# A planner's estimate of TensorE time: a larger charge for each streamed product and each transpose

## The chip, the cores and the metric

The kernel runs on one core of a Trainium2 chip. The core has the engines TensorE (PE, the matrix engine; its loads of stationary operands are shown as PEld), VectorE (DVE), ScalarE (ACT), GpSimd (POOL) and SyncE (SP), and 16 DMA engines. The metric is the device time of one execution in microseconds; less is better.

## What is computed

The reference is a network of two blocks for one sequence of 256 tokens and a width of 2048, in fp32. Cut to its core:

```python
def first_block(x, mem, ...):                      # one layer
    h = rmsnorm(x, g[0])
    y = hybrid_mixer(h, ...)       # h @ w_in; dilated attention, spatial gating, rwkv7 scan; @ w_out
    x = x + rmsnorm(y, g[1])
    h = rmsnorm(x, g[2])
    y = memory_cross_attention(h, rmsnorm(mem, ...), wq, wkv, wo)
    x = x + rmsnorm(y, g[3])
    h = rmsnorm(x, g[4])
    y = conv_ffn(h, ...)           # h @ w_up (11264 columns), conv of width 3, gelu(gate) * val, @ w_down
    return x + rmsnorm(y, g[5])

def second_block(x, c, ctx, c_ctx, ...):           # two layers, tokens x and 256 tokens ctx
    for l in range(2):
        sh_l, sc_l, g_l = split(silu(c) @ w_mod[l] + b_mod[l], 3)       # the modulation; the same for ctx
        hl = xl * (1 + sc_l) + sh_l;  hc = xc * (1 + sc_c) + sh_c
        # hl @ w_in[l], hc @ w_in[l]: short conv, differential attention (softmax - lam * softmax), pool
        out_l = concatenate([y_conv, y_attn, y_pool]) @ w_out[l]
        xl_new = layernorm(ALPHA * xl + g_l * out_l, ...)               # the same for ctx in layer 0
    return xl
```

## The kernel before

**The stream.** All large weights pass once through PE, in the order of the program. They come as pieces of 512 KB (`load_next`, lines 455 to 462, a DMA on SP into a tile `raw`). Each piece is split into two parts: ACT casts it to `whi` (`split_hi`, line 464), DVE subtracts that from the piece and gives `wlo` (`split_lo`, line 472). The activations (`xT`, `yh`/`yl`, `hh`/`hl`, `oT`) are split in the same way. A product of the reference is then three products on PE: whi by both parts of the activation and wlo by the first (`products`, line 535). A moving operand has 256 or 512 columns. A piece is as a rule 24 products. `split_ahead` (line 480) keeps the splits up to three pieces ahead of the products (LK = 3), and the loads up to four pieces ahead of the splits (EK = 4). In a trace all of this stands at line 342, since the class `Engine` passes every instruction through that line; operations are told apart by the names of their tiles.

**The background.** All other work (norms, transposes, attention, rwkv scan, gates, conv, the modulation) is written as Python generators, one queue of them for each lane: a0 to a2 the rwkv chunks, b and c the attention, d the spatial gating, B and C the differential attention, r, t, u and n norms and residuals, w the modulation, and so on. `products` calls `tick` (line 417) after each quarter of a piece, that is after six products. For each lane `tick` emits the next step if the lane's step before has ended by the planner's estimate: `ready[lane] <= clk["P"]`, where `ready` is the estimated end of the last step plus LAG, 0.1 us. The lane w emits a modulation step (on DVE a product and sum `junk` of 1024 columns, and a DMA of `wm`) if DVE's estimated clock is not ahead of PE's by more than WLAG, 0.3 us. `there` (line 426) holds back a step, and a `split_hi`, whose input has not come by the estimate. `until` emits steps without waiting, where the stream itself needs what they make.

**The estimate.** `Meter.note` (line 302) is called for each instruction as it is written. It holds a clock for each engine: an instruction starts at its engine's clock or when its inputs are written and its output is free, if that is later, and ends after `cost` (line 286). The same clocks decide nothing on the chip: they set only the order in which instructions are written into each engine's queue, and the engines execute these queues in order, with semaphores between them.

**Places that are spoken of below.** In the mixer the chunk chain of rwkv: `kn`, `t`, `zrk`, `rl`, `bk`, `ab` are tiles of a chunk on DVE, and `bk<-cons,t` and `bk<-rl,bk` are its small matrix products on PE (a name `bk` also stands for a bank of PSUM). In the second block, `normal0` (line 1981) normalises the rows r of ctx and then of x at the end of layer 0: lane r scales r on ACT (columns 0 to 255) and DVE (the rest); lanes t and n transpose each r on PE (four transposes, `bk<-cons,r`), and ACT then applies scale and shift (`aff<-bk,gb`, two) and casts the two `xT`. The softmax steps of the differential attention (`softmax2`, line 1792) run on ACT (exp into `p`) and DVE (`s`, `p<-p,s,p`), then four transposes `bk<-cons,p` on PE.

Of the kernel before, what the change touches and what calls it, by code (L numbers as in the profile page):

```python
# [10 lines left out]
F32R = mybir.dt.float32r  # L11
# [6 lines left out]
T = 256  # L18
# [250 lines left out]
class Meter:  # L269
# [16 lines left out]
    def cost(s, e, name, aps):  # L286
        n = max(a.free_size() if callable(a.free_size) else a.free_size for a in aps)
        if e == "P":
            if name == "transpose":
                return 0.06  # L290
            o, l, r = aps[:3]
            m, n = l.shape[-1], r.shape[-1]
            return n / 2400 if r.dtype == F32R and n >= T else 4 * max(m, n) / 2400
        return {"V": 0.07 + n / 960, "A": 0.09 + n / 1190, "G": 0.6 + n / 480}[e]

    def table(s, args):
# [1796 lines left out]
```

## Time and profile before

| | us |
|---|---|
| time, median of three runs | 2880.27 (2879.71 to 2881.02) |
| the profiled execution's own time | 2881.7 |
| its span | 2880.0 |
| PE busy | 2831.7 (98%) |
| DVE busy | 2072.1 (72%) |
| ACT busy | 1275.8 (44%) |
| POOL busy | 173.8 (6%) |

The busy time of PE is that of pipelined products whose ends are modelled, so in a stream one reads the distance of their starts. The mean granted clock of PE is 0.993 of full speed over the span; below 1.0 are a few stretches only, near 80 us, near 667 us and at the very end. The order in which the views are read: the page's first part and its chain, the waits of PE, the starts of products in the timeline, and then single stretches.

### The profile page before, as it was taken

To read this page: it belongs to the slowest core of one execution; us is meant where nothing else is said; L and a number is where in the kernel's file an instruction comes from. 1 tells how busy PE (TensorE), PEld (TensorE's weight loads), DVE (VectorE), ACT (ScalarE), POOL (GpSimd) and SP (SyncE) were. 2 spreads that over 40 slices of the span, in tenths; PEclk is the share of its full clock that TensorE was granted. 3 is DMA by queue.
4 is the path that set the end of the run, shared out by engine and by line. 5 is a ranking of instruction groups with operands and counts; after the bars stand their busy time and mean duration, and the time that the engine had idled before them with its cause. 6 is when DMAs were issued, how large, how long until landed. Compare 5 with 4: busy or idle time off the path is not lost.

```text
span 2880.0 us, 53963 instructions
## 1 busy us (share of the span) xinstructions
PE 2831.7 (98%) x22059; PEld 2673.7 (93%) x22059; DVE 2072.1 (72%) x3377; ACT 1275.8 (44%) x2110; POOL 173.8 (6%) x345
## 2 busy tenths in 40 slices
PE   8899999999999999999999999999999999999997
PEld 8789887898999899998899999999999989999996
DVE  6766766787898997888868887885343563776576
ACT  5333335655544445545443554222231463655443
POOL 1001112000000000000100000000010000001001
PEclk9899999999999999999999999999999999999998
DMA  8433337765667886777775334665343453325663
GB/s 268 134 104 105 126 99 251 241 234 187 237 236 242 307 293 223 235 245 271 244 250 179 124 119 169 213 229 182 98 137 117 155 186 107 103 95 182 199 227 132
DMA packets 150857, 538.78 MB, mean 187 GB/s; under 512 B 18240, under 2 KB 18460, under 8 KB 150608
## 3 DMA queue, kind: packets, MB, share of 16 engines
q1 hardware_dynamic: 137808, 494.92, 50.2%
q0 software_dynamic: 12656, 40.37, 5.0%
q8 instruction: 173, 2.83, 0.4%
q14 instruction: 76, 0.62, 0.1%
q10 hardware_dynamic: 144, 0.03, 0.0%
HBM read 528.66 MB, written 6.59 MB: 186 GB/s over the span
## 4 chain that ended last, share of the span: by engine, by line
PE 95%; DVE 2%; DMA 1%; ACT 1%; issue 1%; POOL 0%; SPq 0%; DVEq 0%; ACTq 0%; POOLq 0%
PE acc L342 86%; PE bk L342 10%; DMA raw<-in_w_w_in 1%; DVE wlo L342 1%; ACT whi L342 0%; DVE y L342 0%; DVE res L342 0%; DVE junk L342 0%; DVE zrk L342 0%; ACT junk L342 0%; DVE yg L342 0%; POOL pw L342 0%; POOL R L342 0%; DVE ug L342 0%; DVE zr L342 0%
## 5 line engine op out<-in xcount | busy, mean ns | idle before, releaser
L342 PE MATMUL acc<-xT,whi 128*128 128x256 f32 x8992 | 1581.0, 286 | 13.5 <-ACT whi L342 12.6
L342 PEld LDWEIGHTS acc<-xT,whi 128*128 128x128 f32 x8992 | 1342.1, 192 | 26.6 <-ACT whi L342 13.5
L342 ACT CAST whi<-raw 128x1024 fp32r<-128x1024 f32 x738 | 771.5, 1050 | 906.5 <-PE acc L342 673.0
L342 PE MATMUL acc<-xT,wlo 128*128 128x256 f32 x4496 | 1128.8, 284 | 1.5 <-DVE wlo L342 1.5
L342 DVE TENSOR_TENSOR wlo<-raw,whi 128x1024 fp32r<-128x1024 f32 x738 | 896.8, 1221 | 273.7 <-ACT whi L342 271.2
L342 PEld LDWEIGHTS acc<-xT,wlo 128*128 128x128 f32 x4496 | 800.0, 192 | 2.3 <-DVE wlo L342 2.3
L342 DVE SCALAR_TENSOR_TENSOR junk<-wm,silu 128x1024 bf16<-128x1024 f32 x352 | 421.9, 1220 | 6.3 <-DMA wm<-in_w_mod 5.8
L342 PE MATMUL acc<-whi,xT 128*128 128x256 f32 (+1 forms) x1152 | 284.8, 331 | 0.4 <-ACT xT L342 0.4
L342 PE MATMUL acc<-whi,yh 128*128 128x256 f32 (+1 forms) x768 | 224.5, 319 | 0.0
L342 PEld LDWEIGHTS acc<-whi,xT 128*128 128x128 f32 x1152 | 195.1, 190 | 20.8 <-issue 2.0
L342 PE MATMUL acc<-wlo,yh 128*128 128x256 f32 (+1 forms) x640 | 194.7, 304 | 0.0
L342 PE MATMUL acc<-wlo,xT 128*128 128x256 f32 (+1 forms) x576 | 187.0, 325 | 0.0
L342 PEld LDWEIGHTS acc<-whi,yh 128*128 128x128 f32 x768 | 146.3, 191 | 9.9
L342 PE MATMUL acc<-whi,yl 128*128 128x256 f32 x512 | 144.9, 283 | 0.0
L342 PE MATMUL acc<-wlo,hh 128*128 128x512 f32 x352 | 137.2, 390 | 0.8 <-DVE wlo L342 0.8
L342 PE MATMUL acc<-whi,hh 128*128 128x512 f32 x352 | 137.2, 390 | 0.0
L342 PE MATMUL acc<-whi,hl 128*128 128x512 f32 x352 | 137.0, 389 | 0.0
L342 PEld LDWEIGHTS acc<-wlo,yh 128*128 128x128 f32 x640 | 122.3, 191 | 5.0
L342 PEld LDWEIGHTS acc<-wlo,xT 128*128 128x128 f32 x576 | 109.7, 190 | 7.1
L342 PEld LDWEIGHTS acc<-whi,yl 128*128 128x128 f32 x512 | 98.2, 192 | 0.0
L342 PE MATMUL acc<-whi,oT 128*128 128x512 f32 x256 | 80.6, 392 | 0.6 <-DVE oT L342 0.6
L342 PEld LDWEIGHTS acc<-wlo,hh 128*128 128x128 f32 x352 | 66.1, 188 | 15.0 <-DVE wlo L342 1.5
(347 smaller groups left out, 2612.8 us busy)
## 6 DMA issues: line engine op xcount, KB each, us to landing
raw<-in_w_w_in SPq DMA_DIRECT2D x334, 512.0 KB, 3.6
wm<-in_w_mod SPq DMA_DIRECT2D x192, 512.0 KB, 4.9
raw<-in_w_up SPq DMA_DIRECT2D x176, 512.0 KB, 4.0
raw<-in_w_w_out SPq DMA_DIRECT2D x108, 512.0 KB, 4.4
raw<-in_w_down SPq DMA_DIRECT2D x88, 512.0 KB, 4.7
raw<-in_w_wkv SPq DMA_DIRECT2D x16, 512.0 KB, 5.2
silu<-cond POOLq DMA_DIRECT2D x12, 512.0 KB, 7.7
raw<-in_w_wq SPq DMA_DIRECT2D x8, 512.0 KB, 3.6
```

Source lines behind the costliest of these rows:

```text
L342: return f(*a, **k)
```

## The change

In `cost`, a transpose is charged 0.11 us instead of 0.06, and a product of the stream (fp32r, 256 columns or more) n/2400 + 0.0133 instead of n/2400, so 0.1200 instead of 0.1067 for 256 columns and 0.2266 instead of 0.2133 for 512. The charge of other products (4 x max(m, n)/2400) stays.

```diff
--- before.py
+++ after.py
@@ -287,10 +287,10 @@
         n = max(a.free_size() if callable(a.free_size) else a.free_size for a in aps)
         if e == "P":
             if name == "transpose":
-                return 0.06
+                return 0.11
             o, l, r = aps[:3]
             m, n = l.shape[-1], r.shape[-1]
-            return n / 2400 if r.dtype == F32R and n >= T else 4 * max(m, n) / 2400
+            return n / 2400 + 0.0133 if r.dtype == F32R and n >= T else 4 * max(m, n) / 2400
         return {"V": 0.07 + n / 960, "A": 0.09 + n / 1190, "G": 0.6 + n / 480}[e]
 
     def table(s, args):
```

No instruction of PE, DVE or DMA is added or removed; the order changes. (ACT's queue has two loads of its function tables fewer, 16 where there were 18.) The small products of rwkv, on DVE and PE, in the mixer near 75 to 90 us: `wlo_916`/`wlo_922` belong to `raw_756`, `wlo_946`/`wlo_948` to `raw_825`. DVE before:

```order
L342 TENSOR_TENSOR wlo_904<-raw_726,whi_886 128x1024
L342 TENSOR_TENSOR wlo_916<-raw_756,whi_896 128x1024
L342 TENSOR_SCALAR kn_918<-bk_906 128x4
L342 TENSOR_TENSOR wlo_946<-raw_825,whi_932 128x1024
L342 COPY t_137_806<-kn_918 128x256
L342 TENSOR_SCALAR t_135_804<-t_135_804 128x256
L342 TENSOR_TENSOR wlo_978<-raw_855,whi_964 128x1024
L342 TENSOR_SCALAR t_137_806<-t_135_804,cols,hcol 128x256
L342 TENSOR_TENSOR t_137_806<-zrk_769,t_137_806 128x256
```

DVE now:

```order
L342 TENSOR_TENSOR wlo_908<-raw_726,whi_886 128x1024
L342 TENSOR_SCALAR kn_910<-bk_898 128x4
L342 TENSOR_TENSOR wlo_922<-raw_756,whi_896 128x1024
L342 COPY t_137_806<-kn_910 128x256
L342 TENSOR_SCALAR t_135_804<-t_135_804 128x256
L342 TENSOR_TENSOR wlo_948<-raw_825,whi_932 128x1024
L342 TENSOR_SCALAR t_137_806<-t_135_804,cols,hcol 128x256
L342 TENSOR_TENSOR t_137_806<-zrk_763,t_137_806 128x256
```

COPY t and the t after it moved ahead of the wlo of `raw_825`; they still stand behind that of `raw_756`. PE at the same place, before:

```order
L342 MATMUL acc_794<-xT_322,whi_896 128x256 x2
L342 MATMUL acc_794<-xT_322,wlo_916 128x256
L342 MATMUL acc_794<-xT_322,whi_896 128x256 x2
L342 MATMUL acc_794<-xT_322,wlo_916 128x256
L342 MATMUL bk_980<-cons,t_137_806 128x128 x2
L342 MATMUL acc_795<-xT_322,whi_896 128x256 x2
L342 MATMUL acc_795<-xT_322,wlo_916 128x256
```

PE now:

```order
L342 MATMUL acc_794<-xT_280,whi_886 128x256 x2
L342 MATMUL acc_794<-xT_280,wlo_908 128x256
L342 MATMUL acc_794<-xT_280,whi_886 128x256 x2
L342 MATMUL acc_794<-xT_280,wlo_908 128x256
L342 MATMUL bk_950<-cons,t_137_806 128x128 x2
L342 MATMUL acc_795<-xT_280,whi_886 128x256 x2
L342 MATMUL acc_795<-xT_280,wlo_908 128x256
```

The product `bk<-cons,t` stood six products into the piece of `raw_756` (`whi_896`) and stands now six products into the piece before it (`whi_886`). The next place is ACT in `normal0` for x, at the end of layer 0. Before:

```order
L342 ACTIVATE r_3676_23979<-r_3676_23979,ab_25851 128x256
L342 ACTIVATE aff_25927<-bk_25919,gb_22179 128x256 x2
L342 CAST xT_25928<-aff_25927 128x256
L342 CAST xT_25929<-aff_25927 128x256
L342 CAST whi_25941<-raw_25867 128x1024
L342 ACTIVATE r_3696_24215<-r_3696_24215,ab_25851 128x256
L342 ACTIVATE aff_25953<-bk_25943,gb_22179 128x256 x2
L342 CAST xT_25954<-aff_25953 128x256
L342 CAST xT_25955<-aff_25953 128x256
L342 ACTIVATE r_3714_24447<-r_3714_24447,ab_25851 128x256
L342 CAST whi_25982<-raw_25885 128x1024
```

Now:

```order
L342 ACTIVATE r_3676_23979<-r_3676_23979,ab_25851 128x256
L342 ACTIVATE r_3696_24215<-r_3696_24215,ab_25851 128x256
L342 ACTIVATE aff_25934<-bk_25919,gb_21459 128x256 x2
L342 CAST xT_25935<-aff_25934 128x256
L342 CAST xT_25936<-aff_25934 128x256
L342 CAST whi_25948<-raw_25867 128x1024
L342 ACTIVATE aff_25950<-bk_25927,gb_21459 128x256 x2
L342 CAST xT_25951<-aff_25950 128x256
L342 CAST xT_25952<-aff_25950 128x256
L342 ACTIVATE r_3714_24447<-r_3714_24447,ab_25851 128x256
L342 ACTIVATE aff_25974<-bk_25964,gb_21459 128x256 x2
L342 CAST xT_25975<-aff_25974 128x256
```

Each r came alone between two sets of aff and xT, with a whi beside nearly each of them; now a second r and a second set come before and closer. The last place is DVE in the FFN's up projection, with `U`, `cg`, `cv` the conv's tiles. Before:

```order
L342 TENSOR_TENSOR wlo_8791<-raw_8670,whi_8777 128x1024
L342 SCALAR_TENSOR_TENSOR junk_8815,mpart_5557<-wm_8533,silu_5558 128x1024
L342 TENSOR_TENSOR wlo_8823<-raw_8703,whi_8807 128x1024
L342 SCALAR_TENSOR_TENSOR junk_8849,mpart_5557<-wm_8643,silu_5558 128x1024
L342 TENSOR_TENSOR U_8851<-acc_8575,Rb_7727 128x512
L342 TENSOR_TENSOR U_8852<-acc_8576,Rb_7727 128x512
L342 TENSOR_TENSOR wlo_8865<-raw_8740,whi_8839 128x1024
L342 SCALAR_TENSOR_TENSOR cg_8853<-U_8851,cols,cg_8853 128x255
```

Now:

```order
L342 TENSOR_TENSOR wlo_8847<-raw_8724,whi_8833 128x1024
L342 SCALAR_TENSOR_TENSOR junk_8865,mpart_5557<-wm_8697,silu_5558 128x1024
L342 SCALAR_TENSOR_TENSOR junk_8873,mpart_5557<-wm_8697,silu_5558 128x1024
L342 TENSOR_TENSOR wlo_8881<-raw_8759,whi_8863 128x1024
L342 SCALAR_TENSOR_TENSOR junk_8905,mpart_5557<-wm_8769,silu_5558 128x1024
L342 TENSOR_TENSOR U_8907<-acc_8629,Rb_7761 128x512
L342 TENSOR_TENSOR U_8908<-acc_8630,Rb_7761 128x512
L342 TENSOR_TENSOR wlo_8921<-raw_8798,whi_8897 128x1024
L342 SCALAR_TENSOR_TENSOR cg_8909<-U_8907,cols,cg_8909 128x255
```

Between the same two pieces there stood one `junk` of the modulation; now there are two.

## Rows read from the trace of the kernel before

**Rows 1.** The page: busy time by engine, and the chain that ended last.

```profile
PE 2831.7 (98%) x22059; PEld 2673.7 (93%) x22059; DVE 2072.1 (72%) x3377; ACT 1275.8 (44%) x2110; POOL 173.8 (6%) x345
...
PE 95%; DVE 2%; DMA 1%; ACT 1%; issue 1%; POOL 0%; SPq 0%; DVEq 0%; ACTq 0%; POOLq 0%
```

**Rows 2.** Waits of PE, whole run: waiting engine, releaser, total us, times, longest.

```profile
PE acc L342 <- ACT whi L342: 12.6, 2, 7.0
PE bk L342 <- DVE t L342: 6.2, 1, 6.2
PE bk L342 <- DVE yg L342: 4.6, 4, 3.4
...
PE bk L342 <- DVE y L342: 0.2, 1, 0.2
```

**Rows 3.** Timeline of PE: start, us, engine, operation, count, and idle before it.

```profile
715.99 0.40 PE L342 MATMUL acc<-xT,whi 128*128 128x256 f32 x2
...
716.35 0.40 PE L342 MATMUL acc<-xT,whi 128*128 128x256 f32 x2
...
999.64 0.39 PE L342 MATMUL acc<-wlo,hh 128*128 128x512 f32 x1
999.87 0.39 PE L342 MATMUL acc<-whi,hl 128*128 128x512 f32 x1
```

**Rows 4.** One window: PE, PEld, DVE, ACT, POOL busy, PE's clock, DMA share, GB/s.

```profile
90.00:95.00 5.00, 5.00 (x31) 5.00 (x31) 4.81 (x11) 2.55 (x4) 0.00 (x0) 0.66 0.59 226
```

**Rows 5.** Timeline of PE and then of DVE, 78 to 96 us.

```profile
79.88 0.79 PE L342 MATMUL acc<-xT,whi 128*128 128x256 f32 x2 [5.62 <-ACT whi L342]
...
88.51 1.20 PE L342 MATMUL bk<-cons,t 128*128 128x128 f32 x4 [6.15 <-DVE t L342]
...
90.14 0.63 PE L342 MATMUL acc<-xT,whi 128*128 128x256 f32 x2
...
90.78 0.63 PE L342 MATMUL acc<-xT,whi 128*128 128x256 f32 x2
...
79.86 1.23 DVE L342 TENSOR_TENSOR wlo<-raw,whi 128x1024 fp32r<-128x1024 f32 x1 [10.50 <-ACT whi L342]
81.00 0.15 DVE L342 TENSOR_SCALAR kn<-bk 128x4 f32<-128x4 f32 x1
86.93 1.23 DVE L342 TENSOR_TENSOR wlo<-raw,whi 128x1024 fp32r<-128x1024 f32 x1 [5.78 <-ACT whi L342]
...
91.19 0.41 DVE L342 TENSOR_SCALAR t<-t,cols,hcol 128x256 f32<-128x256 f32 x1
...
95.08 0.42 DVE L342 TENSOR_TENSOR bk<-t,t 64x256 f32<-64x256 f32 x1
```

**Rows 6.** A window in the FFN, with the columns of rows 4.

```profile
720.00:960.00 240.00, 240.00 (x1874) 234.36 (x1874) 215.69 (x305) 119.33 (x146) 1.15 (x2) 1.00 0.71 243
```

**Rows 7.** Timeline of DVE in a softmax step.

```profile
1691.94 1.22 DVE L342 SCALAR_TENSOR_TENSOR junk<-wm,silu 128x1024 bf16<-128x1024 f32 x1
...
1693.08 1.29 DVE L342 TENSOR_REDUCE s<-bk 128x1 f32<-128x512 f32 x2
...
1697.13 0.75 DVE L342 SCALAR_TENSOR_TENSOR p<-p,s,p 128x512 f32<-128x512 f32 x1
```

**Rows 8.** Timeline of PE and then of ACT in normal0 for x.

```profile
2327.05 0.60 PE L342 MATMUL bk<-cons,r 128*128 128x128 f32 x4
2328.89 0.60 PE L342 MATMUL bk<-cons,r 128*128 128x128 f32 x4
...
2327.69 1.02 ACT L342 ACTIVATE aff<-bk,gb 128x256 f32<-128x256 f32 x2 [1.84 <-PE bk L342]
...
2329.21 1.05 ACT L342 CAST whi<-raw 128x1024 fp32r<-128x1024 f32 x1
2330.15 0.60 ACT L342 ACTIVATE r<-r,ab 128x256 f32<-128x256 f32 x1
2330.66 1.01 ACT L342 ACTIVATE aff<-bk,gb 128x256 f32<-128x256 f32 x2
```

## The prediction

> **What bounds the kernel now.** I read the page first: TensorE (PE) is busy 98% of the span and the chain that ended last lies on it for 95% [rows 1]. So only three things can move the time: a wait of PE, a stretch in which PE runs at its lower clock, and work added to PE. The change adds no work to it: the same products and transposes are issued. Then I read the waits of PE [rows 2]: the long ones are 12.6 us on ACT whi (two), 6.2 on DVE t (one) and 4.6 on DVE yg (four), 23.4 together; the ten rows of that view, of which the last has 0.2, sum to 29.1, which is all that a better order could take from waits. Next, whether the new charges are true. In the stream three products of 256 columns start every 0.36 us, 0.12 each, and a product of 512 starts 0.23 after the one before [rows 3]. The old charges were 0.107 and 0.213, the new are 0.120 and 0.227. Four transposes and six products of 512 columns stand between the starts 2327.05 and 2328.89 [rows 8], so the four take 1.84 - 6 x 0.227 = 0.48, which is 0.12 each; charged 0.06 before, 0.11 now. So the planner's PE clock ran some 11% behind PE before and is right now. What hangs on it: a background step is emitted once the estimated end of the step before it (plus LAG) is passed by the PE clock. With a clock that runs faster in estimate, fewer products stand between two steps of a chain on ACT or DVE. The order shows this: between the transposes of two softmax steps stand 48 products where the median was 60, and the separate runs of background work on PE number 309 where they were 293.
>
> **The sum, against the profiled execution (2881.7 us; its span 2880.0; the median of the runs shown is 2880.3, 1.4 below it).** Five terms.
>
> (a) *The starved stretch, 64 to 95 us.* Here PE stands 5.62 us for a whi whose raw piece came late (it starts again at 79.88), and after six products 6.15 us for DVE t [rows 5]. The second wait is a matter of order: on DVE, COPY t stands behind the wlo of the next late piece (86.93), while 18 ready products of the 24 of the piece before stand behind bk<-cons,t on PE. Now COPY t stands one wlo earlier, behind that of 79.86 (after which the next operation begins 1.14 later), and bk<-cons,t is issued 24 products earlier. So PE stops 18 products sooner, 18 x 0.12 = 2.2 us before the old stop at 74.3 (79.88 less 5.62), at 72.1; COPY t comes at 81.0 and PE goes on at 81.3. It then has 42 products. At the low clock three take 90.78 - 90.14 = 0.64; before, work began again at 88.5 and the mean clock of 0.66 in 90 to 95 [rows 4] means half clock up to 93.4, 5 us. So bk<-cons,t and about 21 products go at it, 5 us, and 21 at 0.12, 2.5: PE is at the next piece at about 89. Next late there is bk<-rl,bk, now issued in front of that piece: its inputs are eleven operations of DVE behind the wlo of 86.93, which in the old run take from 91.19 to 95.08 + 0.42, 4.3 us. From 88.07 (the wlo's end) that is 92.4. So PE waits some 3 us and starts the piece at 92.4 and bk<-rl,bk; before, it started it 18 products after the 0.85 of bk<-cons,t from 88.51, at 93.2, and had bk<-rl,bk still to do. **Term: -1** (0.8, and 0.2 of low clock). Bounds -3 (eleven operations at the spacing without that queue) and +5 (PE's clock falls a second time in the new wait: 5 us of half clock, 2.5, and another such wait behind the next late piece).
>
> (b) *The steps of normal0 at the end of layer 0.* ACT works there without a pause: from one aff pair to what follows its two xT 1.52 us, a whi 0.94, an r 0.51 [rows 8], while the planner charges 0.09 + 256/1190 = 0.305 for each operation of 256 columns, so 1.5 for the five of a step that take 2.03. In the old order 6, 9, 12, 12, 12, 9, 12 products of 512 columns stand between the eight groups of transposes of x, 72; now 3, 6, 9, 9, 12, 9, 9, 57. PE goes from the first group to the eighth in 57 x 0.227 + 7 x 0.48 = 16.3 us, before in 19.7. ACT, by its order and from the first group on: 0.64 to the first aff, six aff-and-xT sets 9.1, five r 2.6 (two are done earlier) and four whi 3.8, which is 16.1; at the fifth group it ends at 8.2 where PE comes at 8.05. The eight groups of ctx have 108 products of 256 columns between them where 174 stood: 13.0 + 3.4 = 16.4, and ACT comes out within 0.2 of PE in the same way. **Term: +0.5**, bounds 0 and +4 (each series late by one whi and one set more, 2 us).
>
> (c) *Softmax steps.* The chain from the first s to the end of the last p takes 1697.13 + 0.75 - 1693.08 = 4.8 us [rows 7], and 48 products cover 5.76; 60 covered 7.2. One junk or wlo ahead in DVE's queue costs 1.14 (junk to s, [rows 7]), which makes 5.9, 0.2 too long; two make 7.1, 1.3 too long. There are 40 such steps; I take one in ten with two ahead and let half of these be hidden by other steps: 2 x 1.3 = 2.6 as the upper half, 0 as the lower. **Term: +1**, bounds 0 and +4.
>
> (d) *Short steps of the mixer.* Rwkv and attention steps are placed in quanta of six products, 0.72 us; most stay at 12 products, some fall to 6. No row of before shows such a wait in the steady stream. **Term: +1.5**, two steps late by one quantum, bounds 0 and +4 (six).
>
> (e) *Transitions* between stages (all waits but those on whi and t, 29.1 - 12.6 - 6.2 = 10.3, yg's 4.6 among them [rows 2]). Work that is emitted a little earlier against PE should save part of it; the steps in between are not shorter. **Term: -1.5**, bounds -4 and 0.
>
> Costed at nothing: *the modulation in the FFN.* DVE is busy 215.69 of 240 us [rows 6], 90%. That is the planner's rule seen in the trace: it gives DVE a junk of 1024 columns, charged 1.137 and taking 1.14, whenever DVE's estimated clock is not ahead of PE's, and PE's clock was 11% slow. Now DVE will be filled to nearly 100% until the modulation is done, which comes sooner. What hides it is that a wlo is issued some three pieces (8.6 us) ahead of its products. By the rows' durations DVE falls at most 5 us behind. If that cover goes, the rival below. ACT loads its tables two times fewer; ACT is not on the chain.
>
> Sum: -1 + 0.5 + 1 + 1.5 - 1.5 = +0.5, on the median of 2880.3: **2881 us**.
>
> One rule speaks against the new charge. The rows show 0.120 and 0.227. The Trainium skill, "TensorE: Matmul & The Clock Gate", section "Back-to-back issue gap", gives N/2.4 + 2.5 ns for an isolated product at full clock, an estimate of 0.109 and 0.216, and calls even that too long for a stream of 512 columns (131 ns). By it the new charge would be 10% too long, 48 products would cover 5.2 us instead of 5.76, and term (c) would grow to some +10. The trace does not agree with it here, and the rows decide. For ACT the rows show 0.51 between starts for an r of 256 columns with two column operands. "ScalarE: Activation LUTs", section "What ACT_TABLE_LOAD costs", gives 186 ns + 0.833 N and 93 for each such operand, less an overlap of 93: an estimate of 0.49, which agrees; the planner's 0.305 is what is off, and this rests unchanged.
>
> **Rivals.**
> (1) *Covers too short: slower.* With PE's charge exact and ACT's and DVE's still short (0.305 charged, 0.51 taken), the steps lose the 11% of cover that hid this. For it: ACT without a pause in normal0, the long queue on DVE. Against: the median step of before had over 2 us in hand. Price: normal0 +4, softmax 10 steps x 0.8 = 8, mixer +4, less 1.5 and 1 for (e) and (a): +13.5, 2894. It decides the sign from the point at which the late steps sum to more than the 2.5 us that (a) and (e) give back, and passes the bound of 0.2% at some 8.
> (2) *The starved stretch opens: faster.* If the raw pieces or DVE's inputs come some 3 us sooner with the new order, the new wait stays away and with it the one of 6.15: 6.15 and 1 for the low clock, and 2 more from the transitions: -9, or 2871. For it: the second wait was one of order alone. Against: bk<-rl,bk stands behind a wlo that only a late transfer releases. It decides from the point at which bk<-rl,bk is ready by 89.
> (3) *DVE becomes the bound in the FFN.* If DVE's operations take 3% more than charged, over 480 us that is 14 us, less the 8.6 us of lead: +5.8, 2887. Against: junk charged 1.137 takes 1.14.
> (4) *Nothing to see:* order moves, every wait is replaced by one of its size: 2880 within 3.
>
> **How the numbers follow.** 0.2% is 5.8 us, about what a measurement of this kernel can tell from no change. The forecast, with (4), holds 2875 to 2886 and has a chance of 0.55; rival (1) 0.21, rival (3) 0.06, rival (2) 0.18. So faster by over 0.2% 0.18, within 0.55, slower 0.27. The range runs from 2871.5, the price of (2), to 2893, just short of that of (1), and leaves about 1 in 10 out on each side. The likeliest case's own range is 2875 to 2886.
>
> **What would show it.** In the profile after: one wait of some 9 us on DVE t up to 81 us in place of the waits on whi and t, and one of some 3 on DVE bk up to 92 (a); waits on ACT r or aff below 0.5 us each near the end of layer 0 (b); few waits of a bk on p, in sum under 3 us (c); DVE at 97% or more of the windows 480 to 1000 us and at 60% or less behind, with PE's waits on wlo still in sum under 4 us. The prediction is wrong if PE waits appear in the softmax steps by the dozen, if wlo waits come up in the FFN, or if the low clock spreads to a stretch that ran at 1.00 before.

## The result, and the profile after

The changed kernel takes 2895.68 us (median of five runs, 2893.14 to 2898.49), the kernel before 2880.27 (2879.71 to 2881.02): a ratio of 1.0051, interval 1.004 to 1.0063. It is 15 us slower, and its executions differ by 5 us where those of before differ by 1. The profiled execution (2893.1 us, span 2891.4) is the fastest of the five.

The waits of PE over the whole run, to be set against [rows 2]:

```profile
PE bk L342 <- DVE t L342: 8.7, 1, 8.7
PE acc L342 <- ACT whi L342: 6.7, 1, 6.7
PE bk L342 <- DVE yg L342: 4.5, 4, 3.4
PE bk L342 <- DVE mod L342: 2.7, 1, 2.7
PE acc L342 <- DVE wlo L342: 2.3, 4, 0.8
PE bk L342 <- DVE bk L342: 1.5, 1, 1.5
PE bk L342 <- DVE mq L342: 1.4, 1, 1.4
PE bk L342 <- DVE r L342: 1.0, 3, 0.6
PE bk L342 <- DVE p L342: 1.0, 4, 0.3
```

(Eight smaller rows, 2.8 us together, are left out.) New are mod, bk, r and p; the waits on t and mq grew and one of the two on whi went. All waits together are 33 us, only 4 more than before. So the view of the waits alone does not explain 11 us between the two profiled executions. What does is the start of the same product of the stream in both traces: the 18,672 products stand in the same order in every version, so the difference of two starts, each counted from the beginning of its span, is what was lost up to there. (The last column is the last product; a change within 1 us at a column can be background work that stands on the other side of it.)

| starts, us later | 640th (113 us) | 3000th (656) | 5100th (923) | 6900th (1195) | 7100th (1219) | 8500th (1471) | 11000th (1828) | 15300th (2376) | last |
|---|---|---|---|---|---|---|---|---|---|
| changed - before | 1.2 | 2.3 | 1.6 | 2.9 | 7.3 | 5.3 | 8.3 | 10.7 | 11.2 |
| e1 - before | 5.4 | 7.3 | 7.0 | 8.2 | 10.6 | 8.4 | 9.5 | 9.9 | 10.1 |
| e2 - before | 0.2 | 5.4 | 4.2 | 4.2 | 4.2 | 7.7 | 7.7 | 8.4 | 8.3 |
| e4 - before | 7.7 | 11.1 | 10.5 | 11.6 | 11.8 | 10.0 | 13.1 | 15.5 | 16.0 |
| e7 - before | 6.0 | 13.5 | 13.0 | 13.0 | 13.0 | 10.9 | 11.0 | 11.1 | 11.3 |
| e12 - e11 | 4.7 | 11.7 | 11.2 | 11.2 | 11.2 | 9.3 | 9.3 | 9.4 | 9.6 |
| e13 - e11 | 4.0 | 5.4 | 4.9 | 6.0 | 8.7 | 6.8 | 9.8 | 12.2 | 12.7 |
| e15 - e11 | 4.1 | 3.7 | 3.8 | 3.8 | 3.8 | 3.2 | 3.2 | 3.2 | 3.2 |
| e16 - e11 | 0.6 | 0.6 | 2.0 | 3.8 | 3.8 | 6.1 | 9.1 | 11.5 | 12.0 |
| e14 - e11 | 0.1 | 0.1 | 0.2 | 0.2 | 0.2 | -1.6 | -1.6 | -1.5 | -1.3 |

(The lines of e1 to e16 belong to the experiments below.) In the first line the loss comes in steps: 1.3 in the FFN, 4.3 at one place near 1212 us, 3.0 in the softmax of layer 0, 2.4 in normal0, and 2.0 gained from the FFN's end to the start of the second block. Each step has its place in the trace.

**The modulation's end, 1212 us.** The last steps of the modulation are transposes of `mod` on PE. Timeline of PE, then of DVE (start, us, operation, count, idle before it):

```profile
1211.09 0.28 PE L342 MATMUL acc<-xT,wlo 128*128 128x256 f32 x1
1214.06 0.38 PE L342 MATMUL bk<-cons,mod 128*16 128x128 f32 x1 [2.69 <-DVE mod L342]
...
1211.34 1.22 DVE L342 SCALAR_TENSOR_TENSOR junk<-wm,silu 128x1024 bf16<-128x1024 f32 x1
...
1212.49 1.22 DVE L342 TENSOR_TENSOR wlo<-raw,whi 128x1024 fp32r<-128x1024 f32 x1
1213.63 0.16 DVE L342 TENSOR_TENSOR mod<-mpart 128x16 f32<-128x16 f32 x1
...
1216.54 0.99 DVE L342 SCALAR_TENSOR_TENSOR cg<-U,cols,cg 128x255 f32<-128x255 f32 x2
1217.45 1.00 DVE L342 SCALAR_TENSOR_TENSOR cv<-U,cols,cv 128x255 f32<-128x255 f32 x2
```

DVE has a full queue here and reaches mod some 2.7 us after PE has come to the transpose that needs it. The windows of the FFN say how full that queue is (columns as in [rows 4]; DVE is the third pair, PE's clock the number before the last two):

```profile
720.00:960.00 240.00, 239.19 (x1875) 233.66 (x1874) 231.68 (x338) 116.39 (x144) 1.15 (x2) 1.00 0.77 260
960.00:1210.00 250.00, 250.00 (x1731) 234.43 (x1730) 234.03 (x340) 116.55 (x135) 2.63 (x5) 1.00 0.81 281
1230.00:1330.00 100.00, 100.00 (x748) 96.16 (x748) 68.11 (x89) 54.52 (x72) 3.77 (x7) 1.00 0.62 204
1210.00:1215.00 5.00, 2.31 (x17) 2.11 (x16) 4.93 (x12) 1.12 (x2) 0.00 (x0) 0.86 0.50 176
1215.00:1220.00 5.00, 5.00 (x36) 5.00 (x35) 4.91 (x8) 3.72 (x7) 0.00 (x0) 0.80 0.65 206
```

DVE is busy 231.68 us of 240 where it was 215.69 [rows 6], 97 against 90%, and 68.11 of 100 once the modulation is done. After the wait PE's clock stands below 1.00 in two windows, which makes 4.3 us of a wait of 2.7. DVE is behind its estimate because not every charge of DVE is true. A junk is (1.144 us to the next operation, charged 1.137), but the two operations of cg take 0.91 (1216.54 to 1217.45) where the planner counts 0.73, and 40 such pairs stand between 720 and 960 us: 7 us in 240, or 3%.

**normal0.** PE comes to the transposes of r, and r is not finished (timeline of PE, ACT and DVE, layer 0's end; before, [rows 8]):

```profile
2312.01 0.27 PE L342 MATMUL bk<-cons,r 128*128 128x128 f32 x1
2312.83 0.55 PE L342 MATMUL bk<-cons,r 128*128 128x128 f32 x3 [0.55 <-DVE r L342]
...
2344.74 0.66 PE L342 MATMUL bk<-cons,r 128*128 128x128 f32 x4
...
2344.07 0.61 ACT L342 ACTIVATE r<-r,ab 128x256 f32<-128x256 f32 x1
...
2310.56 0.76 DVE L342 TENSOR_TENSOR xT<-aff,xT 128x256 fp32r<-128x256 f32 x2 [0.74 <-ACT xT L342]
...
2311.24 1.22 DVE L342 TENSOR_TENSOR wlo<-raw,whi 128x1024 fp32r<-128x1024 f32 x1
2312.37 0.41 DVE L342 TENSOR_SCALAR r<-r,ab 128x256 f32<-128x256 f32 x1
```

The r that the group of 2344.74 needs begins on ACT at 2344.07 and takes 0.61: it ends 0.06 before. That group loses 0.25 us. The three groups that lose most (those of 2312.01, 2350.65 and 2353.62, 1.7 together) wait for DVE's part of r instead: DVE stands 0.74 us for an xT of ACT, takes a wlo, and comes to r at 2312.37 only. **Softmax.** The same on DVE, where a junk stands before the first reduction; the transposes of p break in two (timeline of DVE, then PE). Before, a junk stood there too [rows 7]; what is new is that fewer products follow.

```profile
1675.46 1.22 DVE L342 SCALAR_TENSOR_TENSOR junk<-wm,silu 128x1024 bf16<-128x1024 f32 x1
...
1676.61 1.28 DVE L342 TENSOR_REDUCE s<-bk 128x2 f32<-128x512 f32 x2
...
1681.59 0.41 PE L342 MATMUL bk<-cons,p 128*128 128x128 f32 x2
...
1682.28 0.44 PE L342 MATMUL bk<-cons,p 128*128 128x128 f32 x2 [0.28 <-DVE p L342]
```

Four transposes that took 0.48 with the way in and out take 1.24, and the view of the waits counts only 0.28 of it. Of the 24 steps of layer 0 seven are late, by 0.07 to 0.91 us, which makes the 3.0.

**The starved stretch.** PE stands once, on t, until 81.03, and then 1.5 us on bk (PE, then DVE; before, [rows 5]):

```profile
81.03 1.19 PE L342 MATMUL bk<-cons,t 128*128 128x128 f32 x4 [8.70 <-DVE t L342]
90.97 1.16 PE L342 MATMUL bk<-rl,bk 64*128 64x128 f32 x8 [1.48 <-DVE bk L342]
...
91.29 0.42 DVE L342 TENSOR_TENSOR bk<-t,t 64x256 f32<-64x256 f32 x1
```

### The profile page after: what moved, and what is told of

Same layout as the page of the kernel before. It is cut to its first block, busy times and chain, and to the rows that moved or that the text cites. A ratio compares the mean times of both kernels' runs of the same rounds, so it can differ in the third digit from the quotient of the medians.

```text
span 2891.4 us, 53960 instructions
## 1 busy us (share of the span) xinstructions
PE 2838.8 (98%) x22059; PEld 2674.1 (92%) x22059; DVE 2067.6 (72%) x3377; ACT 1273.2 (44%) x2108; POOL 181.7 (6%) x345
## 5 line engine op out<-in xcount | busy, mean ns | idle before, releaser
L342 DVE SCALAR_TENSOR_TENSOR junk<-wm,silu 128x1024 bf16<-128x1024 f32 x352 | 420.7, 1218 | 11.5 <-DMA wm<-in_w_mod 10.6
L342 PEld LDWEIGHTS acc<-whi,xT 128*128 128x128 f32 x1152 | 195.1, 190 | 21.4 <-issue 2.7
```

Source lines behind the costliest of these rows:

```text
L342: return f(*a, **k)
```

## The experiments

Theory A: each step of a chain had more products in front of it than its chain took, only because PE was charged too little; with PE right and ACT and DVE still charged too little, the steps come late. Theory B: it is the modulation alone, which now fills DVE. Theory C: any other order costs so much. Theory D: the loss is in the starved stretch. Times are medians with the lowest and highest; ratios are against the kernel before on the same chip.

**The two halves, e1 and e2.**

```diff
-                return 0.11        # e1: transposes back
+                return 0.06
-            return n / 2400 + 0.0133 if ...        # e2: products back
+            return n / 2400 if ...
```

> Only the product's charge (n/2400 + 0.0133); a transpose is charged 0.06 as before. Theory A (each place loses cover, because products that stood between two steps of a chain are gone): nearly the whole loss, since all covers are counted in products: 2892 to 2896, with the waits on mod near 1214 us, on p in the softmax steps and on r in normal0. Theory B (DVE filled up by the modulation): the same, since the products are what moves PE's clock in the FFN. Theory C (chance of the order: any other order moves the time by so much, either way): anything between 2875 and 2895, with waits at other places.

> Only the transpose's charge (0.11); a product is charged n/2400 as before. Theory A: a step with four transposes loses 0.2 us of cover, a tenth of what the products take: 2880 to 2883. Theory B: no transposes stand in the FFN, so nothing: 2880. Theory C: anything between 2875 and 2895.

e1: 2892.31 (2890.55 to 2895.22), ratio 1.0041, with 2.1 us on mod. e2: 2890.03 (2887.65 to 2894.66), ratio 1.0035, without a wait on mod or p, and 0.2 us on r. By theory A the transposes should have cost 1 us and cost 9: in e2's trace 4.2 before the FFN, 2.7 of them at a wait of 2.0 on ACT oT, and 3.5 at the start of the second block (a wait of 2.3 us on ACT xT). The halves sum to 20 where both together cost 15. e1 has the time that A gave, but not the places: 7.0 of its 10.1 us are lost before the FFN, 1.1 in the softmax and 0.4 in normal0, with no wait on r. So cover counted in products explains mod in e1, and it explains neither e2 nor the mixer; this miss is only partly cleared up below.

**The modulation, e3 and e4.** e3 lets the modulation fill DVE to 90% only, by a second clock; e4 puts the transposes of mod off.

```diff
+                s.v2 = max(s.v2, t) + 1.11 * c                      # e3, for each DVE operation
-        if ... not s.quiet and m["V"] <= m["P"] + WLAG:
+        if ... not s.quiet and s.meter.v2 <= m["P"] + WLAG:
+        t1 = s.meter.last + 4.0                                     # e4, after mod's additions
-            while not s.fits("w"):
+            while not s.fits("w") or (s.meter.clk["P"] < t1 and not s.force):
```

> Both new charges, but the modulation's steps are placed by a second estimate of DVE's clock that charges each DVE operation 11% more, so that DVE is not filled beyond 90% by them. Theory A: the wait on mod (2.7 us and the low clock after it, 4.3 in all) and the wait on wlo in the FFN (1.0) go, the rest stays: about 2890. Theory B: all goes: about 2881. Theory C: anything.

> Both new charges; the transposes of mod on PE are put off until PE's estimated clock is 4 us past the end of mod's additions. Theory A: that wait alone goes, 4.3 us with the low clock after it, of which some 1 is lost again at the end of the FFN: 2891 to 2892. Theory B: the same 4 us here, and nothing else. Both theories say that DVE's queue near 1214 us stays some 3 us behind. If the time stays at 2895, the wait on mod was covered later by other slack.

e3: 2890.45 (2889.45 to 2895.24), ratio 1.0038; no wait on mod; p grew to 2.2, and the wait on wlo at the FFN's end to 2.0. e4: 2890.98 (2888.88 to 2897.96), ratio 1.0033. The medians fall by 5 us, as theory A says, though the executions of both overlap with those of the changed kernel; B falls: two thirds of the loss stay. e4's profiled execution was its slowest, and its order is that of the changed kernel up to the end of the modulation. Yet it is 8.8 us later at the 3000th product (table, 11.1 against 2.3). The waits of one order differ that much: in e4 PE stands 3.05 us on bk, and then its clock falls a second time (one row of PE's timeline, and two windows):

```profile
92.98 2.07 PE L342 MATMUL bk<-rl,bk 64*128 64x128 f32 x8 [3.05 <-DVE bk L342]
```

```profile
90.00:95.00 5.00, 2.02 (x9) 1.80 (x9) 4.87 (x13) 3.65 (x4) 0.00 (x0) 0.78 0.55 206
95.00:100.00 5.00, 5.00 (x21) 4.55 (x21) 3.76 (x6) 0.00 (x0) 0.00 (x0) 0.50 0.64 206
```

**Other sizes of the product's charge, e5 and e6** (n/2400 - 0.0133 and n/2400 + 0.0010, transposes 0.06).

> The opposite of the change: a product is charged 0.0133 less than in the kernel before (n/2400 - 0.0133), a transpose 0.06 as before. Theory A (cover): every step has still more products in front of it than before, so no wait that the changed kernel shows: 2876 to 2881. Theory C (the time of any other order scatters upwards of that of before): 2885 to 2895, with waits at places that have nothing to do with cover.

> A product is charged 0.001 more than in the kernel before (a thirteenth of the change), a transpose as before. The covers shrink by under 1%. Theory A: 2880 to 2882. Theory C: the order differs all the same, so 2885 to 2895. Bears also on the starved stretch: if bk<-rl,bk waits there with the clock at 1.00 the time is low, if the clock falls a second time some 5 us more.

e6: 2878.85 (2877.82 to 2880.29), ratio 0.9991 (0.9982 to 0.9999): an order with no loss, which speaks against theory C. It is a weak test: only 735 of the 3387 background instructions of PE stand behind another number of products than before, against 3211 in the changed kernel. e5: 2903.53 (2901.25 to 2906.01), ratio 1.0075. More cover is no gain either, which A did not say. Its largest step is 15.5 us at the FFN's end (PE, then DVE):

```profile
1320.30 0.79 PE L342 MATMUL acc<-wlo,hh 128*128 128x512 f32 x1 [12.39 <-DVE wlo L342]
...
1302.86 1.21 DVE L342 SCALAR_TENSOR_TENSOR junk<-wm,silu 128x1024 bf16<-128x1024 f32 x1
...
1316.91 1.22 DVE L342 SCALAR_TENSOR_TENSOR junk<-wm,silu 128x1024 bf16<-128x1024 f32 x1
...
1319.03 2.35 DVE L342 TENSOR_TENSOR wlo<-raw,whi 128x1024 fp32r<-128x1024 f32 x2
```

With PE's clock slower still in the estimate the modulation got too few steps, was not done when the second block needed it, and its last 12 junks (of which the first and the last are shown) were emitted in a row, ahead of the next wlo. The pace of the modulation has a limit on both sides.

**More cover by LAG, e8, and truer charges, e7** (LAG = 0.6; and):

```diff
+        c = ...                                   # the number of operands of one column
+        if e == "A" and name == "activation":
+            return 0.11 + n / 1190 + 0.09 * c
+        if e == "V" and name in ("scalar_tensor_tensor", "tensor_tensor_scan"):
+            return 0.13 + n / 960
```

> The changed kernel with truer charges for the other engines too (an ACT activation 0.11 + n/1190 and 0.09 for each column operand, a DVE scalar_tensor_tensor or scan 0.13 + n/960), and the transposes of mod put off by 4 us as in e4. Theory A (cover): the covers are right again, so the waits on p, r and wlo go: softmax 3, normal0 2.4, mod 4.3 and wlo 1 less than the changed kernel, 2883 to 2886 with the scatter of the starved stretch. Theory B (the modulation on DVE alone): mod and wlo go, the waits on p and r stay: 2889 to 2891.

> The changed kernel with LAG 0.6 instead of 0.1: a background step is emitted half a microsecond of PE later after the step before it. Theory A: the waits on p in the softmax steps and on r in normal0 go (each was 0.2 to 0.7 us), those on mod and wlo stay, since the modulation's lane does not use LAG: 5 us less, about 2890. Theory B: nothing gained, 2895. If longer chains make a stage's end late, waits at the ends of stages take the place of these.

e8: 2899.99 (2897.91 to 2902.46), ratio 1.0062. The waits on p and r fell only from 2.0 to 1.3 together, and new ones came (xT 2.8, oT 1.9, st 1.2): half a microsecond for every step is no substitute for a charge where it belongs. e7: 2892.76 (2890.8 to 2893.75), ratio 1.0036. The sum missed A's by 7, but not where A speaks: from the 5100th product on e7 loses nothing in the FFN, softmax and normal0 and gains 2.1 at the second block; it is 13 us late before the FFN. The wait of 14.3 us on t is not what makes it late, since e6 has it too and loses nothing. Most of it is one wait on a wlo that DVE reaches behind a row of rwkv operations, and the clock after it (PE, DVE and two windows; before, the clock is 1.00 here):

```profile
328.84 0.79 PE L347 MATMUL acc<-wlo,xT 128*128 128x512 f32 x1 [4.30 <-DVE wlo L347]
...
327.06 0.42 DVE L347 TENSOR_TENSOR bk<-t,t 64x256 f32<-64x256 f32 x1
...
327.57 3.49 DVE L347 TENSOR_TENSOR wlo<-raw,whi 128x1024 fp32r<-128x1024 f32 x3
```

```profile
330.00:335.00 5.00, 5.00 (x20) 4.31 (x19) 3.61 (x5) 0.37 (x1) 0.00 (x0) 0.50 0.86 284
335.00:340.00 5.00, 5.00 (x19) 4.32 (x19) 2.71 (x6) 0.00 (x0) 0.00 (x0) 0.50 0.06 22
```

With 0.55 in the window behind these, 7.2 us of clock are lost, and 4.3 in the wait: 11.5 of the 13. e12 has the same wait (4.2 us), without the starved stretch. So in the mixer the truer charges let the wlo come too late and make it worse than PE's charges alone do (11.7 against 3.7, e12 and e15 at the 3000th product).

**The starved stretch, e9 to e12.** Both versions cut the store brow<-dil, e9 and e10 by head into 12 stores of one partition each, e11 by copied row into 8 stores of 12 partitions (shown). e10 is the changed kernel with e9's stores, e12 is e7 with e11's.

```diff
-        nc.gpsimd.dma_start(s.brow[:, :, :], w[0:12, 0:383].unsqueeze(1).to_broadcast([12, P, 383]))
+        for h in range(8):
+            t0 = s.meter.clk["P"] + 14.0
+            nc.gpsimd.dma_start(brow[:, 16 * h:16 * h + 16, :], w[0:12, 0:383].unsqueeze(1).to_broadcast([12, 16, 383]))
+            yield 0
+            while s.meter.clk["P"] < t0:
+                yield 0
```

> The kernel before, but the store brow<-dil (issued at 52.9 us, 35 us on its way, first read at 251 us) is cut into 12 stores, one for each head, at least 8 us apart by the planner's PE clock. If that store starves the raw loads at 64 to 95 us, the waits there (12.2 us) and most of the half clock (some 8 us) go: 2863 to 2868, and the time scatters no more than before. If the transfers are short there for another reason: 2880.

> The changed kernel with the same 12 stores. If the starved stretch makes its scatter (2893 to 2898: the clock falls a second time in some executions), the executions come within 2 us of each other. Theory A: what is left against the kernel before with 12 stores is cover lost at mod (4.3), wlo (1), softmax (3) and normal0 (2.4), less 2 at the end of the FFN: 9 us, so 2873 to 2877. Theory B: 4 to 5 us. Theory C: another order once more, any difference.

> The kernel before with the store brow<-dil cut along its 128 copied rows into 8 stores from all 12 partitions, some 9 us or more apart. In e9, each of the 12 stores read one partition and held the DMA engines near 1.0 with 50 GB/s, so the raw loads starved all the same. If the store is what starves them, the time on the DMA engines is 4 us in 9 now and raw loads pass between: the waits on whi and t at 70 to 90 us shrink from 14 to under 6, 2868 to 2875. If not, the waits stay and the time is 2880.

> e7 and e11 together. Theory A with a store that starves the loads: as far below e7 as e11 is below the kernel before, 2870 to 2877, with little scatter. If the order alone makes the starved stretch long or short, no such sum holds.

e9: 2881.94 (2878.88 to 2889.36), nothing gained; e10: 2904.31 (2902.43 to 2905.62), with a new wait of 10.9 us on ACT bt in the mixer, whose cause was not followed. e11: 2865.74 (2864.9 to 2866.03), ratio 0.9943 (0.993 to 0.9955); e12: 2876.32 (2874.1 to 2878.3), 0.9981. One window of e9 and one of e11 (DMA share and GB/s are the last two numbers):

```profile
60.00:65.00 5.00, 4.49 (x38) 4.29 (x37) 4.82 (x12) 1.42 (x2) 0.00 (x0) 1.00 1.09 55
```

```profile
65.00:70.00 5.00, 5.00 (x42) 4.85 (x41) 3.54 (x6) 2.32 (x4) 0.00 (x0) 1.00 0.86 300
```

The spacing held in part only, since the estimate decides on it: in e9's trace three stores are issued within 2.7 us (52.98, 54.92, 55.69) and are on their way together until 63 to 76 us; in e11's two within 2.1 us, which land by 63.1, and the next at 72.5. So e9 is no test of one store at a time: three of one partition each held the DMA engines and moved 55 GB/s with the loads. And the 300 GB/s of e11 belong to a window with no store on its way; beside its first two stores the windows from 55 to 65 us show 100 and 124. What decides is how long loads stand beside a store: the raw piece issued at 56.7 us took 22.0 us before, and the one of 56.4 took 7.5 in e11. In e11 the wait on t and the second wait on whi are gone, 15.9 us in the trace between the 450th and the 640th product: the store starved the loads, which the prediction took as given.

**The change without that stretch, e13 to e18,** all with e11's stores. e13: both charges; e15: both up to the FFN's first group, the old ones after; e16: the reverse; e14: as e16, with e7's charges and e4's delay; e18: e14 without the delay (it turned out to be the same order as e14, see below); e17: e14 with n/2400 + 0.0010 before the FFN.

```diff
-                return 0.06
+                return 0.11 if s.late else 0.06          # e16; s.late is set at group "up0"
-            return n / 2400 if ...
+            return n / 2400 + (0.0133 if s.late else 0.0) if ...
```

> Both charges of the change on the kernel with 8 stores (e11, 2865.7 us), where the starved stretch is gone. Theory A (lost cover, place by place as in the trace of the changed kernel): wlo in the FFN 1.1, mod 4.3, softmax 3.0, normal0 2.4, second layer 0.4, less 2.0 at the start of the second block, 9.2 in all, and some 1 in the mixer: 2875 to 2877, executions within 2 us of each other. Theory D (most of the loss is the starved stretch, which the old order happens to pass well): 2866 to 2870.

> e11 with both new charges up to the FFN's first group and the old ones from there. Theory A and D: with the starved stretch gone the mixer loses what its short steps lose, 0 to 3 us: 2866 to 2869. If the mixer loses more than 5, as e7 and e2 did in their profiles, the loss there is of the order and not of the starved loads.

> e11 with the old charges up to the FFN's first group and both new charges from there. Theory A: the 9.2 us of the places in the FFN and the second block, 2874 to 2876; e15 and e16 sum to e13. Theory D: 2866 to 2868.

> e11 with the old charges up to the FFN's first group and from there the charges of e7 (PE's new ones, truer ones for ACT and DVE, the transposes of mod 4 us later). Theory A: from there on e7 lost nothing and won 2.2 at the start of the second block, so 2863 to 2864.5, the fastest so far. If the win of 2.2 hangs on the order of the mixer before it: 2865.7.

> e14 without the delay of mod's transposes. If DVE's queue is behind near the end of the modulation because its scalar_tensor_tensor operations were charged 0.06 too little each, the truer charges keep it from falling behind and the wait on mod is under 1 us: 2863 to 2866. If the queue is behind because the modulation's lane fills DVE at all, the wait stays at 2 to 3 us with the low clock after it: 2866 to 2869.

> e14 with the product's charge raised by 0.001 (as in e6) up to the FFN's first group, where e14 has the old one. Theory A: the covers of the mixer change by under 1%; e6's profile was 1.6 us shorter than that of the kernel before up to there, but through the starved stretch, which is gone here: 2862 to 2866, no difference that can be measured from e14.

Against e11's 2865.74: e13 2878.75 (2877.17 to 2881.27), 13.0 more; e15 2870.26 (2868.02 to 2871.39), 4.5; e16 2878.2 (2875.47 to 2880.68), 12.5; e14 2863.84 (2863.35 to 2864.78), 1.9 less. Theory D falls: without the stretch 13.0 of the 15 us are still lost, in the traces 7.3 from the FFN on, at the places of theory A, and 5.4 before it, where A had given 1 (table). The halves sum to 17: in e16 the FFN loses 7.6 us (3.2 up to the 7100th product, 4.4 at a later end of the modulation), in e13 3.8. e13's waits, in which t and bk have gone and A's four remain:

```profile
PE bk L342 <- DVE mod L342: 2.3, 1, 2.3
PE acc L342 <- DVE wlo L342: 1.9, 3, 0.8
...
PE bk L342 <- DVE r L342: 1.0, 3, 0.6
PE bk L342 <- DVE p L342: 1.0, 4, 0.3
```

In e14 there is no row of mod, r or p, and the only one of wlo is

```profile
PE acc L348 <- DVE wlo L348: 1.0, 2, 0.5
```

Only ACT's and DVE's charges and the delay of mod are new against e16, and the 12.5 us are gone; 599 of the 871 background instructions of PE from there on stand elsewhere than before, so another order need not cost anything there, and from the FFN on theory C falls. In the mixer it does not: every run here that moves most of the 2516 background instructions there is 2 to 17 us late at the 3000th product, e5 with its longer covers too.

e18 takes 2864.41 (2863.28 to 2866.0). It is not a second experiment: in the traces of e14 and e18 the instructions of PE, DVE, ACT and POOL stand in the same order, so the delay changed nothing, and the charges alone did it. In both, the transpose of mod comes 11 us after mod is done (1283.07 and 1294.47 in e18): by the planner's clocks the conv's operations put DVE ahead of PE just then, and the lane w had to wait. DVE had also caught up shortly before: 6 us ahead of mod it stood idle for a whi of ACT (DVE, then PE, in e18).

```profile
1276.39 1.23 DVE L348 TENSOR_TENSOR wlo<-raw,whi 128x1024 fp32r<-128x1024 f32 x1 [0.50 <-ACT whi L348]
...
1282.90 0.17 DVE L348 TENSOR_TENSOR mod<-mod,cols 128x16 f32<-128x16 f32 x1
...
1294.47 0.27 PE L348 MATMUL bk<-cons,mod 128*16 128x128 f32 x1
```

Why DVE keeps up is not shown. The charge 0.13 + n/960 mends most of that of the conv (a pair is counted as 0.85 now and takes 0.91), but it charges a junk 1.197, and a junk still takes 1.144. For the 70 junks between 720 and 960 us that is 3.7 us too much, nearly what the charge mended for the conv's 36 pairs gives (0.12 each, 4.3). So part of the cure is that the modulation runs slower, as in e3 (mod is done at 1283 us, in e16 at 1241). No run separates the two, nor ACT's charges from DVE's. The fastest is e17, 2862.81 (2861.78 to 2863.75), ratio 0.9937 (0.9924 to 0.9951), 18 us below the kernel before on the same chip.

## Why the prediction was wrong

It said 2881 and no change, with 2871.5 to 2893; 2895.7 lies above. Rival (1) had the mechanism at most of the places from the FFN on, at a chance of 0.21. That its 2894 came so near is partly luck: its 8 us in the softmax stand for 3.0, its 4 in normal0 for 2.4, and the 5.6 us of the modulation and its wlo are not in it. For these rival (3) was the nearer one (chance 0.06): its condition, DVE 3% slower than charged, is about what the trace shows, and only the wait was another. It was put aside because a junk takes its charge, which the operations of the conv do not. Step by step:

- **The charges are right now** held, and what it does to the order too (fewer products between steps).
- **(a), -1.** The shape was as told: one wait of 8.7 us up to 81.0 (forecast 9 to 81.3), then one on bk up to 91 (1.5; forecast 3 up to 92.4). The size was too good for most executions. The bound of "+5, the clock falls a second time" is what e4's trace shows. Over the medians the stretch costs 15.4 - 13.0 = 2.4; in the profiled execution, the fastest, it gains instead (1.2 at the 640th product, with e13 - e11 at 4.0).
- **(b), +0.5, measured 2.4.** The hand sum had ACT level with PE within 0.2 us and took level as free; and it counted ACT alone. Six of the sixteen groups were late by more than 0.1 us, and the three that lost most waited for DVE's part of r, for which the sum had no term.
- **(c), +1, measured 3.0.** It was right that 48 products are 0.2 us too few with one junk in the way, but it priced two in the way, at two steps of the 40. Seven steps of layer 0 were late, by 0.43 on the mean, the step shown above with one junk in the way and the operations of another lane among its own.
- **(d), +1.5, measured about 5** (e13 - e11 at the 3000th product, 5.4, of which 0.2 stands before the 450th). In e13's trace PE has 185 separate runs of background work up to there, 171 in e11. The two ends of a run take 0.13 us more than two starts inside stream and background: 14 x 0.13 is about 2. The rest is not followed; short waits that e11 lacks (mq, tab, t, rl, pp) are part of it.
- **(e), -1.5, measured -2.0** at the one transition where work came earlier to a gain, from the FFN's end to the second block's start. The other long one, yg, kept its 4.5 us.
- **"Costed at nothing: the modulation in the FFN"** is the step that failed as a step, and the largest: put at 0, it cost 5.6 us, 1.3 with the wait on wlo and 4.3 at mod. The forecast that DVE fills up was right (97%, and 68.11 of 100 us once the modulation was done). What hides it was named for wlo alone, three pieces of lead. The modulation's own last operations, transposes on PE, have no lead: its lane emits them as soon as DVE's estimated clock is level with PE's, so PE arrives just after mod should be done, and waits for all that DVE is behind its estimate.

Of the signs that the prediction named, nearly all came true (the one wait on t up to 81 us, p under 3 us, DVE at 97%, wlo under 4), with the time 15 us off: they were sums of waits, and the waits show 4 us of the 11.

Behind the steps from the FFN on stands one omission. The prediction found ACT's charges 0.2 short of 0.51 and noted that this "rests unchanged". But the errors were not independent: PE's clock 11% slow gave each chain the cover that ACT's and DVE's missing charges took. Mending one alone took the cover away (e16, 12.5 us); e14 raises the others too, from the FFN on, and loses nothing. For the mixer this account is not shown: there e14 keeps the old charges, and e12, with all of them raised, loses more. The products' time held: in the changed kernel's FFN three start every 0.36 us too (1201.13, 1201.49, 1201.85).

What stays open: why transposes alone (e2) bring the waits on oT and xT and cost 9 us, of which cover in products explains little; what makes most of the 5 us of the mixer; and whether e14 wins by charges that are true or by the junks that are now charged too much.

## What to carry to other kernels

Before a wrong number in a planner is corrected, list the other wrong numbers that it pays for: correct the charges of all engines on a chain together, or give the chain its slack openly. Try it stage by stage: here it paid from the FFN on and cost 11 us in the mixer. When background work is sped up, follow each operation that it issues, on every queue, to the last one; the instructions at its end, on the engine that bounds the kernel, may have no lead at all. And measure a loss by the start of the same stream instruction in both traces: the view of the waits showed 4 us of 11.

## What the runs showed of the hardware

One store of 2.3 MB from 12 partitions, each read 128 times, was 35 us on its way, and raw loads of 512 KB beside it took 22.0 and 21.4 us (issued at 56.7 and 64.4 us; the DMA engines moved 74 to 160 GB/s in the windows from 60 to 85 us). Three stores of 192 KB from one partition each, on their way at once, held the DMA engines at a share of 1.09 with 55 GB/s moved, loads included. With eight stores of 287 KB from 12 partitions, a load beside two of them took 7.5 us, and one with no store on its way 3.5 (issued at 64.2 us). A wait of 2.7 us on PE in a stretch at full clock cost 4.3, since the clock's mean in the five microseconds after it was 0.80. A wait of 3.05 us soon after a longer one brought 0.50, the lower of the two levels, and so did one of 4.3 us by itself (e7: 0.50 in the two profile windows after it, 1.00 there in the kernel before).
